# Recurrent blocks of a hybrid decoder layer: gates, recurrence and block end issued inside the next block's u projection, with the block's gate projection kept in another PSUM bank

## The chip, the cores and the metric

The kernel runs on one core of a Trainium2 chip. The metric is the device time of one execution in microseconds (us). The core has five engines with queues of their own: TensorE (PE in the profile, its weight loads PEld), VectorE (DVE), ScalarE (ACT), GpSimd (POOL) and SyncE (SP). Each works through its own instructions in order; semaphores hold an instruction back until what it reads is there, or until the place it writes is free. In this kernel SP's queue carries the loads of weights, POOL's the small transfers between stages.

## The reference

One layer over 16 meta positions and 1024 tokens, width 2048, all in float32. The input is normalized and multiplied by one wide matrix, the parts of which feed an attention branch and a recurrent branch; both are gated, joined, projected out, added to the input and normalized.

```python
h = rmsnorm(x, norm_g[l], NORM_EPS)
proj = jnp.einsum('btd,de->bte', h, w_in[l])
q, k, v, g_att, u, g_lru = jnp.split(proj, splits, axis=-1)
...
att = diff_attention(q, k, v, dist_bias, lam)           # softmax1 @ v - lam * softmax2 @ v, causal, 8 heads
att = (rmsnorm(att, subln_g[l], SUBLN_EPS) * (1.0 - lam_init)).reshape(B, T, D_ATTN)
att = att * jax.nn.silu(g_att)
rec = rg_lru_branch(u, ...)
rec = rec * jax.nn.silu(g_lru)
x = x + jnp.einsum('bte,ed->btd', jnp.concatenate([att, rec], axis=-1), w_out[l])
```

The recurrent branch works on 8 blocks of 128 channels:

```python
u = causal_depthwise_conv4(u, conv_w) + conv_b
r = jax.nn.sigmoid(u_block @ w_a + b_a)                 # gate r
i = jax.nn.sigmoid(u_block @ w_x + b_x)                 # gate i
a = jnp.exp(-LRU_C * r * jax.nn.softplus(-lru_lambda))
b = jnp.sqrt(-jnp.expm1(2.0 * log_a)) * i * u           # 1 in place of the root at t = 0
h[t] = a[t] * h[t - 1] + b[t]
```

## The kernel before

**Precision.** A float32 product is made of three fast matmuls. Each operand is split into a rounded high part and the rest (`split`, L77 to L80: the high part by ACT, the rest by DVE), and high x high, high x low and low x high are added up in PSUM. So each step over 128 rows of the contraction is a group of three matmuls (L158 to L160), and weights arrive as a load by SP (`wraw`, 2 buffers), a copy by ACT (`whi`, 3 buffers) and a subtraction by DVE (`wlo`, 3 buffers), each of half a column block (128 x 1024).

**Stages.** The sequence is worked in two halves: half A (meta positions and the first 512 tokens, 528 columns) and half B (512 columns). The stages follow each other on PE: attention of half A (8 heads, to about 450 us of the span), the 8 recurrent blocks of half A (to about 642 us, while POOL, ACT and DVE prepare the input of half B), attention of half B (to about 1141 us), the 8 recurrent blocks of half B (to about 1308 us), and the output projection.

**One head.** `head` (L225) projects q and k, makes scores (tag S, L339 and L341), takes the two softmaxes and their difference (L346 to L365, ending in DVE's L364), projects v and the gate, and then transposes the probabilities (L396, tag T), splits them (L400, L404) and multiplies by v into one bank, `pv` (L401 to L407). The bank is copied out (`att`, L413), its squares are summed by two matmuls into the same bank again (`ms`, L418 and L419), and the head ends in a store by POOL.

**One recurrent block.** `lru` (L523) gives two projections, u and gr, each 48 matmuls per column chunk (half A has two chunks for u, 272 and 256 columns). As soon as u is there, the sink `u_sink` (L450) calls `finish` (L464): four convolution steps on DVE (`uc`), the split into `uh` (ACT) and `ul` (DVE), the gate products (L485 to L487: 12 matmuls in half A, 6 in half B, into tags S and T), two sigmoids, a chain of ACT and DVE work, and the scan. After gr's 48 matmuls, `g_sink` (L509) scales it, takes its sigmoid, multiplies with the scan's result and stores by POOL.

**Order.** The Python code issues the blocks one after the other; a list scheduler with a model of the engines then sets the order on every engine from the dependences, and gives tiles their places when it issues them. `issue_after` holds what is issued within it behind an instruction on the same engine. `proj` (L135) has an argument `midway`: a function that is called before the ninth of the 16 groups of a chunk, with the rest of the chunk held behind the instruction that it returns. Before the change only the first head used it.

**PSUM.** Eight banks: tag S has 3, T has 2, proj has 2, and pv has 1. Before, u and gr of a recurrent block take tag proj (T in block 1 of half B), and pv lies idle while the recurrent blocks run.

## Time and profile before

| | |
|---|---|
| time, median of 3 runs | 1640.6 us (1637.65 to 1643.15) |
| profiled execution | 1637.0 us, of which the span is 1635.2 |
| TensorE busy | 1596.9 us, 98 % of the span, 8466 matmuls |
| DVE, ACT, POOL busy | 1117.6, 874.1, 205.2 us |
| mean granted TensorE clock | 0.995 |

The span runs from the first instruction to the last; the rest of the execution lies around it. Busy shares of PE count overlapping matmuls once. Since PE is busy nearly throughout, a stretch is read by its PE idle time: what PE waited for, where, and what the other engines did just before.

### The profile page before, as it was taken

What the parts mean: (1) busy time and instruction counts of PE and PEld (TensorE: products, weight loads), DVE (VectorE), ACT (ScalarE), POOL (GpSimd) and SP (SyncE); (2) the same over time, 40 slices, a digit from 0 to 9 for tenths busy, and PEclk for the clock granted to TensorE, in tenths of its full rate; (3) what the DMA queues carried; (4) which work ended last, traced back from release to release, by engine and by line L of the source; (5) the groups of instructions that cost most, each with busy time, mean ns of one, the idle gap of its engine ahead of it and who ended that gap; (6) DMA issues with size and microseconds to landing.
All of it is one profiled execution on the core that took longest, in us unless ns stands there. A gap on an engine that the chain in (4) does not pass through costs nothing.

```text
span 1635.2 us, 22985 instructions
## 1 busy us (share of the span) xinstructions
PE 1596.9 (98%) x8466; PEld 1370.8 (84%) x8466; DVE 1117.6 (68%) x2218; ACT 874.1 (53%) x1392; POOL 205.2 (13%) x308
## 2 busy tenths in 40 slices
PE   7999999999999999999999999999999999899996
PEld 6889889998989888888888888887887887788885
DVE  6766556665676667667668667757877656867996
ACT  5655555545566657456556556545776543332533
POOL 1211111110011010201011001000000002200262
PEclk9999999999999999999999999999999999999999
DMA  9633344333344443533234234233443388969874
GB/s 310 206 121 109 116 137 132 122 124 108 122 146 145 145 142 123 183 114 116 84 120 134 78 120 123 78 97 100 138 138 114 120 309 290 326 234 330 307 283 154
DMA packets 85196, 261.61 MB, mean 160 GB/s; under 512 B 11659, under 2 KB 13748, under 8 KB 84956
## 3 DMA queue, kind: packets, MB, share of 16 engines
q1 hardware_dynamic: 60544, 192.18, 35.2%
q0 software_dynamic: 24304, 67.90, 12.6%
q8 instruction: 67, 1.10, 0.3%
q14 instruction: 45, 0.37, 0.1%
q10 hardware_dynamic: 236, 0.06, 0.0%
HBM read 213.35 MB, written 39.86 MB: 155 GB/s over the span
## 4 chain that ended last, share of the span: by engine, by line
PE 75%; DVE 8%; issue 7%; DMA 7%; ACT 3%; POOL 1%; SPq 0%; ACTq 0%; DVEq 0%; POOLq 0%
PE proj L158 20%; PE proj L159 19%; PE proj L160 19%; PE T L396 2%; PE o L685 2%; PE o L686 2%; PE o L684 2%; DVE wlo L80 2%; PE S L341 2%; PE S L339 2%; DMA wb<-w_out 1%; DVE y L700 1%; DVE wb L658 1%; DMA xb<-mix_d 1%; DMA xt<-x 1%
## 5 line engine op out<-in xcount | busy, mean ns | idle before, releaser
L158 PE MATMUL proj<-hTA,whi 128*128 128x256 f32 (+2 forms) x1152 | 373.5, 325 | 1.9 <-ACT whi L79 1.9
L159 PE MATMUL proj<-hTA,whi 128*128 128x256 f32 (+2 forms) x1152 | 370.4, 322 | 0.0
L160 PE MATMUL proj<-hTA,wlo 128*128 128x256 f32 (+2 forms) x1152 | 369.5, 322 | 0.5 <-DVE wlo L80 0.5
L79 ACT ACTIVATE whi<-wraw 128x1024 fp32r<-128x1024 f32 (+1 forms) x218 | 228.2, 1047 | 244.8 <-PE proj L159 186.6
L80 DVE TENSOR_TENSOR wlo<-wraw,whi 128x1024 fp32r<-128x1024 f32 (+1 forms) x218 | 264.0, 1212 | 116.5 <-ACT whi L79 116.3
L158 PE MATMUL proj<-hTB,whi 128*128 128x512 f32 x768 | 302.1, 393 | 1.2 <-DVE gr L291 0.6
L160 PE MATMUL proj<-hTB,wlo 128*128 128x512 f32 x768 | 300.9, 392 | 0.0
L159 PE MATMUL proj<-hTB,whi 128*128 128x512 f32 x768 | 299.8, 390 | 0.0
L158 PEld LDWEIGHTS proj<-hTA,whi 128*128 128x128 f32 x1152 | 218.8, 190 | 18.7 <-ACT whi L79 2.6
L160 PEld LDWEIGHTS proj<-hTA,wlo 128*128 128x128 f32 x1152 | 218.7, 190 | 16.3 <-DVE wlo L80 0.7
L159 PEld LDWEIGHTS proj<-hTA,whi 128*128 128x128 f32 x1152 | 219.0, 190 | 14.4
L685 PE MATMUL o<-wlo,mix 128*128 128x512 f32 x416 | 163.2, 392 | 7.9 <-DVE wlo L80 7.9
L158 PEld LDWEIGHTS proj<-hTB,whi 128*128 128x128 f32 x768 | 144.3, 188 | 30.4 <-DVE gr L291 2.6
L160 PEld LDWEIGHTS proj<-hTB,wlo 128*128 128x128 f32 x768 | 144.2, 188 | 30.1
L159 PEld LDWEIGHTS proj<-hTB,whi 128*128 128x128 f32 x768 | 144.3, 188 | 28.6
L686 PE MATMUL o<-whi,mix 128*128 128x512 f32 x416 | 162.6, 391 | 0.0
L684 PE MATMUL o<-whi,mix 128*128 128x512 f32 x416 | 162.5, 391 | 0.0
L358 ACT ACTIVATE s<-s,st 128x144 f32<-128x144 f32 (+7 forms) x128 | 100.0, 782 | 50.9 <-DVE st L356 50.1
L685 PEld LDWEIGHTS o<-wlo,mix 128*128 128x128 f32 x416 | 78.4, 189 | 26.4 <-DVE wlo L80 10.0
L351 DVE TENSOR_SCALAR_CACHE_REDUCE s<-S,b 128x256 f32<-128x256 f32 (+5 forms) x176 | 82.6, 477 | 19.4 <-PE S L341 16.2
L684 PEld LDWEIGHTS o<-whi,mix 128*128 128x128 f32 x416 | 78.5, 189 | 16.6 <-ACT gate L488 0.3
L686 PEld LDWEIGHTS o<-whi,mix 128*128 128x128 f32 x416 | 78.5, 189 | 16.2
(240 smaller groups left out, 2357.6 us busy)
## 6 DMA issues: line engine op xcount, KB each, us to landing
wraw<-w_in SPq DMA_DIRECT2D x190, 512.0 KB, 4.0
wraw<-w_out SPq DMA_DIRECT2D x48, 512.0 KB, 4.3
mix<-mix_d SPq DMA_DIRECT2D x48, 256.0 KB, 5.1
wb<-w_out SPq DMA_DIRECT2D x24, 512.0 KB, 5.1
t_d<-wb POOLq DMA_DIRECT2D x16, 512.0 KB, 6.8
xb<-mix_d SPq DMA_DIRECT2D x24, 256.0 KB, 6.4
kk_d<-kk POOLq DMA_DIRECT2D x8, 528.0 KB, 3.0
kk<-kk_d POOLq DMA_DIRECT2D x8, 528.0 KB, 4.1
```

Of the source, the lines that this page charges most:

```text
L79: nc.scalar.activation(hi, src, AF.Copy)
L80: nc.vector.tensor_tensor(out=lo, in0=src, in1=hi.bitcast(F32), op=ALU.subtract)
L158: nc.tensor.matmul(ps[:, :n], lhsT=hi[:, c], rhs=xh, start=(kt == 0), stop=False)
L159: nc.tensor.matmul(ps[:, :n], lhsT=hi[:, c], rhs=xl, start=False, stop=False)
L160: nc.tensor.matmul(ps[:, :n], lhsT=lo[:, c], rhs=xh, start=False, stop=(kt == KT - 1))
L339: nc.tensor.matmul(ps[:, :w], lhsT=qq[:, j, qc], rhs=kk[:, j, c0:c0 + w], start=True, stop=False)
L341: nc.tensor.matmul(ps[:, :w], lhsT=self.qz[:, j, qc], rhs=kl[:, c0:c0 + w], start=False, stop=True)
L351: nc.vector.tensor_scalar(out=s[j][:, a:a + n], in0=ps[:, a - c0:a - c0 + n], scalar1=self.b31[:, h:h + 1], scalar2=-3.0e38, op0=ALU.add, ...
L358: nc.scalar.activation(s[j][:, :s_len], s[j][:, :s_len], AF.Exp, bias=nm[:, j:j + 1], accum_out=l[:, j:j + 1])
L684: nc.tensor.matmul(acc, lhsT=x[:, 0, tk], rhs=w[0], start=start, stop=False)
L685: nc.tensor.matmul(acc, lhsT=x[:, 0, tk], rhs=w[1], start=False, stop=False)
L686: nc.tensor.matmul(acc, lhsT=x[:, 1, tk], rhs=w[0], start=False, stop=stop)
```

## The change

`proj` now calls its `midway` function in the first of its chunks only. In `lru_part` the old `finish` is cut in two: `convolve` (convolution and split, still called as soon as u is there) and `recur` (gates, recurrence). `g_sink` now only keeps gr's bank, and a new `finish` runs `recur` and then what `g_sink` did; it returns the last gate matmul. The loops over blocks hand this `finish` as `midway` to the next block's u projection, so that a block's gates, recurrence and end are issued before the ninth group of the next u, and the rest of that u is held behind the last gate matmul. The last block's `finish` follows by itself. gr has to wait in PSUM for that long, and takes tag pv, which has one bank.

```diff
@@ -148,2 +148,3 @@
         for unit in work:
+            hook, midway = midway, None
             acc = [self.ps.tile([P, 512], F32, tag=j[3], name="proj", bufs={"S": 3, "pv": 1}.get(j[3], 2)) for _, j in unit]
@@ -151,4 +152,4 @@
                 for kt in range(KT):
-                    if kt == 8 and midway:
-                        order.enter_context(self.tc.issue_after(midway().ins))
+                    if kt == 8 and hook:
+                        order.enter_context(self.tc.issue_after(hook().ins))
                     c = slice((kt % 8) * P, (kt % 8) * P + P)
@@ -460,6 +461,6 @@
                 if c0 + w == n:
-                    state["h"] = finish()
+                    convolve()
             return f
-        def finish():
+        def convolve():
             ue = state["ue"]
@@ -476,2 +477,6 @@
                 nc.vector.tensor_copy(out=carry[:, 0:3], in_=ue[:, n:n + 3])
+            state["u"] = uc, uh, ul
+
+        def recur():
+            uc, uh, ul = state["u"]
             gates = []
@@ -486,3 +491,3 @@
                     nc.tensor.matmul(ps[:, :w], lhsT=wh, rhs=ul[:, c], start=False, stop=False)
-                    nc.tensor.matmul(ps[:, :w], lhsT=wl, rhs=uh[:, c], start=False, stop=True)
+                    last = nc.tensor.matmul(ps[:, :w], lhsT=wl, rhs=uh[:, c], start=False, stop=True)
                     nc.scalar.activation(o[:, c], ps[:, :w], AF.Sigmoid, bias=par[:, 5 + g:6 + g])
@@ -506,5 +511,11 @@
                 nc.vector.tensor_copy(out=carry[:, 3:4], in_=d[:, n - 1:n])
-            return d
+            state["h"] = d
+            return last
         def g_sink(ps):
+            state["g"] = ps
+
+        def finish():
+            last = recur()
+            ps = state["g"]
             sg = pool.tile([P, HALF], F32, tag="sg", name="sg", bufs=1)
@@ -519,6 +530,8 @@
             self.emit_mix(half, H + b, sg)
+            return last
+
+        return u_sink, g_sink, finish
-        return u_sink, g_sink
+    def lru(self, b, half, pool, tl, hT, tag="proj"):
-    def lru(self, b, half, pool, tl, hT, tag="proj", g_tag="proj"):
         gw = self.lru_weights(b, pool)
@@ -528,6 +541,6 @@
             self.carry[b] = self.carry_all[:, 4 * b:4 * b + 4]
-        us, gs = self.lru_part(b, half, pool, tl, gw, self.carry[b])
+        us, gs, finish = self.lru_part(b, half, pool, tl, gw, self.carry[b])
         chunks = [(0, HALF)] if half else [(0, 272), (272, 256)]
         return ((M_U + b, [(hT, c0, w, tag, us(c0, w)) for c0, w in chunks]),
-                (M_GR + b, [(hT, 0 if half else META, HALF, g_tag, gs)]))
+                (M_GR + b, [(hT, 0 if half else META, HALF, "pv", gs)]), finish)
@@ -853,5 +866,7 @@
             step, squares, fin_b = self.prep(pb, nc.gpsimd, self.xb, HALF, 1, hTB, LA, 2)
+            finish = None
             for b in range(8):
-                for m, jobs in self.lru(b, 0, pool, pool, hTA):
-                    self.proj((m, jobs))
+                u, g, then = self.lru(b, 0, pool, pool, hTA)
+                for m, jobs in (u, g):
+                    self.proj((m, jobs), midway=finish if m < M_GR else None)
                     if m < M_GR:
@@ -861,2 +876,4 @@
                             squares(b)
+                finish = then
+            finish()
             fin_b()
@@ -876,5 +893,7 @@
         with tc.tile_pool(name="lruB", bufs=1, side="left", reuse_waits="tile") as pool:
+            finish = None
             for b in range(8):
-                for m, jobs in self.lru(b, 1, pool, tl, hTB, *("T" if b == 1 else "proj",) * 2):
-                    self.proj((m, jobs))
+                u, g, then = self.lru(b, 1, pool, tl, hTB, "T" if b == 1 else "proj")
+                for m, jobs in (u, g):
+                    self.proj((m, jobs), midway=finish if m < M_GR else None)
                     if 1 <= b < 5:
@@ -883,2 +902,4 @@
                                 mixA.append(self.load_mix(m1, 0, len(mixA)))
+                finish = then
+            finish()
         tail.close()
```

The lines of the changed kernel are some lines further down (the projection's three matmuls are L159 to L161, the gates L490 to L492, the transposes L397, ms L419 and L420). Three places show what the scheduler makes of it.

First, PE at the gates of a block in the middle of half A (block 4 of 8, counted from 0). Before, the gates stand behind six matmuls of what follows (`proj<-hTA_1...` is group 1 of 16), first the four with `uh`, then those with `ul`:

```order
L159 MATMUL proj<-hTA_1_177,whi 128x272
L160 MATMUL proj<-hTA_1_161,wlo 128x272
L485 MATMUL S<-uh,lwh 128x272
L485 MATMUL S<-uh,lwh 128x256
L485 MATMUL T<-uh,lwh 128x272
L485 MATMUL T<-uh,lwh 128x256
L158 MATMUL proj<-hTA_2_162,whi 128x272
L159 MATMUL proj<-hTA_2_178,whi 128x272
L160 MATMUL proj<-hTA_2_162,wlo 128x272
L486 MATMUL S<-ul,lwh 128x272
```

In the changed kernel they stand behind 24 matmuls of the next block's u (`hTA_7` is group 7), twelve in a row:

```order
L159 MATMUL proj<-hTA_7_167,whi 128x272
L160 MATMUL proj<-hTA_7_183,whi 128x272
L161 MATMUL proj<-hTA_7_167,wlo 128x272
L490 MATMUL S<-uh,lwh 128x272
L491 MATMUL S<-ul,lwh 128x272
L492 MATMUL S<-uh,lwl 128x272
L490 MATMUL S<-uh,lwh 128x256
L491 MATMUL S<-ul,lwh 128x256
L492 MATMUL S<-uh,lwl 128x256
L490 MATMUL T<-uh,lwh 128x272
```

So the gates come 18 matmuls of 272 columns later after gr than before, and nothing else stands among them.

Second, PE at the end of the last attention head of half B. `s_10793` and `s_10821` are the probabilities of the last two of four row tiles, `proj<-hTB_15` is the end of block 0's u, and `hTB_0` to `hTB_2` in the piece of before are the start of its gr:

```order
L159 MATMUL proj<-hTB_15_4896,whi 128x512
L160 MATMUL proj<-hTB_15_4880,wlo 128x512
L158 MATMUL proj<-hTB_0_4865,whi 128x512
L159 MATMUL proj<-hTB_0_4881,whi 128x512
L160 MATMUL proj<-hTB_0_4865,wlo 128x512
L158 MATMUL proj<-hTB_1_4866,whi 128x512
L159 MATMUL proj<-hTB_1_4882,whi 128x512
L160 MATMUL proj<-hTB_1_4866,wlo 128x512
L158 MATMUL proj<-hTB_2_4867,whi 128x512
L159 MATMUL proj<-hTB_2_4883,whi 128x512
L396 MATMUL T<-ident,s_10793 16x128
L160 MATMUL proj<-hTB_2_4867,wlo 128x512
```

Now:

```order
L160 MATMUL proj<-hTB_15_4896,whi 128x512
L161 MATMUL proj<-hTB_15_4880,wlo 128x512
L397 MATMUL T<-ident,s_10793 16x128
L397 MATMUL T<-ident,s_10740 128x128
L397 MATMUL T<-ident,s_10765 128x128
L397 MATMUL T<-ident,s_10793 128x128
L397 MATMUL T<-ident,s_10821 16x128
L397 MATMUL T<-ident,s_10821 128x128
L402 MATMUL pv<-pm,vv 128x512
L406 MATMUL pv<-pth,vv 128x512
```

Before, the 48 matmuls of gr stand among the transposes of the last two row tiles; in the changed kernel gr uses the bank that pv and ms still hold, and stands only after the gates of block 0. Nothing but attention is left on PE from here to the last pv.

Third, ACT between the last pv and block 0's gates in half B. `pth_11091` is the split of the squares that ms reads, `sq_11090` a logarithm of ms, `uh_11191` what the gates read, `mix_...` a stored half-A result loaded back by SP and split. Before:

```order
L79 ACTIVATE mix_11386<-mix_11386 128x512
L79 ACTIVATE pth_11091<-sq_11090 128x512
L79 ACTIVATE mix_11390<-mix_11390 128x512
L79 ACTIVATE lwh_11118<-lw_11116 128x256
L79 ACTIVATE mix_11462<-mix_11462 128x512
L79 ACTIVATE mix_11466<-mix_11466 128x512
L79 ACTIVATE whi_11477<-wraw_11476 128x1024
L79 ACTIVATE mix_11571<-mix_11571 128x512
L79 ACTIVATE mix_11575<-mix_11575 128x512
L79 ACTIVATE lwh_11287<-lw_11285 128x256
L79 ACTIVATE whi_11483<-wraw_11482 128x1024
L79 ACTIVATE uh_11191<-uc_11186 128x512
```

Now:

```order
L79 ACTIVATE pth_11082<-T_11080 128x128
L414 ACTIVATE att_11089<-pv_10993 128x512
L79 ACTIVATE whi_11269<-wraw_11268 128x1024
L79 ACTIVATE pth_11091<-sq_11090 128x512
L79 ACTIVATE mix_11364<-mix_11364 128x512
L79 ACTIVATE mix_11368<-mix_11368 128x512
L79 ACTIVATE lwh_11118<-lw_11116 128x256
L79 ACTIVATE mix_11433<-mix_11433 128x512
L79 ACTIVATE mix_11437<-mix_11437 128x512
L422 ACTIVATE sq_11090<-eg_10583 128x512
L79 ACTIVATE uh_11191<-uc_11186 128x512
```

The splits of `mix` and of gate weights (`lwh`) stand ahead of `uh` in both; `whi_11269`, which takes the place of the first half of block 1's u weights, now stands ahead of `pth_11091`. The loads on SP that go with it (`wraw` are weights, `mix` the stored results), before:

```order
L118 DMA wraw_11394<-w_in 128x1024
L118 DMA wraw_11400<-w_in 128x1024
L118 DMA wraw_11476<-w_in 128x1024
L619 DMA mix_11386<-mix_d0_0_119 128x512
L619 DMA mix_11390<-mix_d0_1_120 128x512
L619 DMA mix_11462<-mix_d0_2_121 128x512
```

And SP in the changed kernel:

```order
L118 DMA wraw_11372<-w_in 128x1024
L632 DMA mix_11364<-mix_d0_0_119 128x512
L632 DMA mix_11368<-mix_d0_1_120 128x512
L118 DMA wraw_11378<-w_in 128x1024
L632 DMA mix_11433<-mix_d0_2_121 128x512
L632 DMA mix_11437<-mix_d0_3_122 128x512
```

So `mix_11433` is now loaded behind `wraw_11378`, which takes the buffer of `wraw_11268`, the source of `whi_11269` and of the `wlo` beside it. On PE the two `ms` matmuls and the gates now follow the 24th matmul of block 1's u, with nothing between them.

## Rows read from the trace of the kernel before

**Rows 1.** Page, busy time of each engine over the whole execution

```profile
PE 1596.9 (98%) x8466; PEld 1370.8 (84%) x8466; DVE 1117.6 (68%) x2218; ACT 874.1 (53%) x1392; POOL 205.2 (13%) x308
```

**Rows 2.** Busy time by stretch: width, PE, PEld, DVE, ACT, POOL, clock, DMA share, GB/s

```profile
1117.00:1160.00 43.00, 41.63 (x197) 33.30 (x196) 28.73 (x50) 24.39 (x38) 2.19 (x4) 1.00 0.37 121
```

**Rows 3.** Waits of PE over the whole span: total us, times, longest

```profile
PE S L485 <- ACT uh L79: 3.9, 4, 2.2
...
PE S L486 <- DVE ul L80: 0.7, 3, 0.2
```

**Rows 4.** Order of time on PE, gates of block 4, half A: start, duration, releaser

```profile
561.27 0.29 PE L159 MATMUL proj<-hTA,whi 128*128 128x272 f32 x1
561.39 0.28 PE L160 MATMUL proj<-hTA,wlo 128*128 128x272 f32 x1
563.84 0.51 PE L485 MATMUL S<-uh,lwh 128*128 128x272 f32 x2 [2.16 <-ACT uh L79]
```

**Rows 5.** Order of time on ACT, the same place

```profile
561.16 1.06 ACT L200 ACTIVATE xt<-xt 128x1024 f32<-128x1024 f32 x1 [1.53 <-DMA xt<-x]
...
562.21 1.04 ACT L79 ACTIVATE whi<-wraw 128x1024 fp32r<-128x1024 f32 x1
563.16 0.63 ACT L79 ACTIVATE uh<-uc 128x528 fp32r<-128x528 f32 x1
```

**Rows 6.** Busy time by stretch, around the gates of block 4

```profile
561.30:563.80 2.50, 0.38 (x4) 0.16 (x2) 2.05 (x5) 2.50 (x5) 0.00 (x0) 1.00 0.00 0
...
564.80:568.30 3.50, 3.28 (x16) 3.12 (x15) 2.83 (x5) 3.49 (x7) 0.00 (x0) 0.51 0.51 167
```

**Rows 7.** Order of time on PE, one gate wait of half B

```profile
1237.83 0.74 PE L485 MATMUL S<-uh,lwh 128*128 128x512 f32 x2 [1.05 <-ACT uh L79]
```

**Rows 8.** Order of time, all engines, start of the first recurrent block, half A

```profile
452.11 0.40 PE L158 MATMUL proj<-hTA,whi 128*128 128x512 f32 x1
...
452.19 1.06 ACT L79 ACTIVATE whi<-wraw 128x1024 fp32r<-128x1024 f32 x1 [1.12 <-PE proj L159]
...
453.49 1.22 DVE L80 TENSOR_TENSOR wlo<-wraw,whi 128x1024 fp32r<-128x1024 f32 x1
```

**Rows 9.** Order of time, all engines, last softmax of half B to its pv

```profile
1120.27 0.39 PE L158 MATMUL proj<-hTB,whi 128*128 128x512 f32 x1
...
1124.12 1.30 DVE L364 SCALAR_TENSOR_TENSOR s<-s,st,s 128x1040 f32<-128x1040 f32 x1
...
1130.75 0.38 PE L396 MATMUL T<-ident,s 128*16 128x128 f32 x2
...
1131.42 0.39 PE L159 MATMUL proj<-hTB,whi 128*128 128x512 f32 x1
...
1131.65 0.40 PE L160 MATMUL proj<-hTB,wlo 128*128 128x512 f32 x1
...
1133.01 0.50 PE L401 MATMUL pv<-pm,vv 80*128 80x512 f32 x1 [0.96 <-DVE pm L88]
```

**Rows 10.** Order of time, all engines, end of the last pv to ms

```profile
1146.16 0.28 PE L407 MATMUL pv<-pth,vv 128*128 128x128 f32 x1
...
1146.47 0.60 ACT L413 ACTIVATE att<-pv 128x512 f32<-128x512 f32 x1 [4.90 <-PE pv L407]
...
1147.11 0.69 DVE L414 TENSOR_TENSOR sq<-att 128x512 f32<-128x512 f32 x1 [3.94 <-ACT att L413]
...
1148.84 1.22 DVE L80 TENSOR_TENSOR wlo<-wraw,whi 128x1024 fp32r<-128x1024 f32 x1
...
1150.53 0.83 SPq L619 DMA_DIRECT2D mix<-mix_d  x2
...
1150.88 0.62 ACT L79 ACTIVATE pth<-sq 128x512 fp32r<-128x512 f32 x1
...
1151.70 0.74 DVE L470 SCALAR_TENSOR_TENSOR uc<-ue,lru_par_sb,uc 128x512 f32<-128x512 f32 x1
...
1154.81 1.23 ACT L79 ACTIVATE mix<-mix 128x512 fp32r<-128x512 f32 x2 [0.49 <-DMA mix<-mix_d]
```

## The prediction, made before the changed kernel was run

> **What bounds the kernel now.** I read the page first: TensorE is busy 98 % of the span and the other engines far less [rows 1], so a change in the order can only win or lose the time in which PE stands still. The windows by stage come next: from the last scores of half B to the first gates PE is busy 41.63 of 43.00 us, at a clock of 1.00 [rows 2]. Then the waits of PE: the gate matmuls wait 3.9 us for `uh` in four places (the longest 2.2) and 0.7 us for `ul` in three [rows 3]. The order of time shows how the longest arises. After the last u matmul at 561.39 nothing is issued until the first gate matmul at 563.84 [rows 4]. On ACT, which works in order, a square of `xt` and a weight copy `whi`, 1.06 and 1.04 us, stand ahead of `uh` [rows 5]. So the gates are ready to run about two microseconds too early in PE's order, six matmuls into the next u.
>
> **The gates in the steady blocks.** The change puts them behind 24 matmuls of the next u, 18 later than before. By rows 4 a wait of 2.45 us from issue to issue is the worst; 18 matmuls of 272 columns, at 0.12 us from issue to issue (561.27 to 561.39 [rows 4]), are 2.2 us. `uh` also stands ahead of the square on ACT then, and the waits for `ul`, 0.2 us at most, vanish with it. In half B the gates move behind 24 matmuls of 0.23 us (1131.42 to 1131.65 [rows 9]), 5.5 us, where the one wait in the rows was 1.05 [rows 7]. I take all 4.6 us of rows 3 as gone. Issue to issue a wait costs a little more than the view shows (2.45 less one matmul of 0.12 is 2.33, where it says 2.16), 0.16 over seven waits: 1.1 more.
>
> With the longest wait goes something else. In the 3.5 us from 564.80 the granted clock is 0.51, which is 1.2 GHz of the two levels, after 2.45 us with hardly a matmul at 1.00 [rows 6]; half of the work is lost there, 3.5 x (1 - 0.51) = 1.7 us. The sum of the gain: 4.6 + 1.1 + 1.7 = **7.4 us**; should `uh` still be late in half A's worst block, as rows 4 leave 0.1 us open, it is less by the price of that. The steady blocks pay nothing for the bank: gr's result is read by the first DVE instruction behind gr (the multiplication that gives `gx`, no longer behind the scan's chain in the order), and the next gr comes a whole u later.
>
> **The start of the recurrent blocks, half A.** Block 0's gr can't follow its u any more, since pv and ms of the last head hold the bank. PE goes on with block 1's u instead, whose first weights take the buffer of the half that PE has just finished. In the row of before that same copy starts at 452.19 and takes 1.06, the subtraction beside it ends at 453.49 + 1.22 = 454.71, and PE would have been through at 452.11 [rows 8]. In that time PE can run four u matmuls of 0.12 and one ms matmul of 0.23, 0.7 us in all. Of the 2.6 us to 454.71 it loses **1.9**. Before, gr's weights lay ready. At the other ends (the last block of half A, and of half B before the output projection) the gates follow the 48 matmuls of gr at once, 11 us after u, and `uh` has long been made: 0. POOL's store of a block's result moves half a u later, and the loads queued behind it on POOL feed work that PE needs only in the next stage: 0.
>
> **The end of attention, half B.** This is the dear part. Before, the last head's softmax, its transposes and its pv products had 48 matmuls of gr among them; now these are blocked by the bank, and of block 1's u only the first 24 may run before block 0's gates.
> - PE has finished block 0's u and can go to the transposes at 1120.27; the four that it can do take under half a microsecond, to about 1120.7. The last difference of softmaxes ends at 1124.12 + 1.30 = 1125.42 [rows 9]. Wait: 4.7.
> - From the last small transposes to the first pv product pass 1133.01 - 1130.75 = 2.26 us, in which ACT and DVE copy and split. Before, three gr matmuls filled a part, so PE lost 1133.01 - 1131.65 less one matmul of 0.23, that is 1.13 [rows 9]. Now one transpose is left to fill it: 2.0, so +0.9. The rest of the pv chain waits as before.
> - After the last pv product follow six u matmuls, 1.4 us. For ms come, by the rows of before: a gap of 0.31 to `att`, 0.60, `sq` 0.69 with its gap of 0.04, which is 1.6; then the weight copy `whi` that now stands ahead, 1.06, which starts only when the six u matmuls are through (1.8), ends at 2.9; then `pth`, 0.62 [rows 10]: 3.5 after the last pv, so PE waits 2.1. The second ms matmul needs `ptl`, behind `wlo` (1.22), a convolution step (0.74) and itself as long as `sq` (0.69) [rows 10]: at 2.9 + 2.65 = 5.5; with ms's first matmul done at 3.7 PE waits another 1.8.
> - The gates need `uh`. Ahead of it on ACT stand splits of stored half-A results. The load of the third stands on SP behind a weight load that needs the buffer free, so after `wlo` at 4.1; before, such a pair was issued at 1150.53 and used at 1154.81, 4.28 us later [rows 10]. That gives 4.1 + 0.4 + 4.3 = 8.8; two splits take 1.23, a logarithm and `uh` 0.6 each: 11.2. PE is through with ms at 5.7 and waits 5.5, and 0.2 for `ul`, as the waits of before had at most [rows 3].
>
> The sum is 4.7 + 0.9 + 2.1 + 1.8 + 5.5 + 0.2 = **15.2 us**. Of these I can bound the last: if the load were there at once, ACT and DVE alone (four splits of 0.6, `lwh` 0.4, the chain of ms behind `ptl`) bring `uh` at about 9.4, and PE waits 3.7. Upward nothing in the rows bounds the load; I allow 1 us. So 13.4 to 16.2.
>
> **The clock after such waits.** No row shows a wait of 4.7 or 5.5 us in the middle of PE's work. After 2.45 us with little work the level fell to 1.2 GHz for 3.5 us and cost 1.7 [rows 6]; after the gap of 1.36 us at 1131.65 [rows 9] the window shows no fall [rows 2]. By these I take one full price for the gates' wait, 1.7, and 0.7 for the softmax's wait, since the pv chain behind it stands partly on ACT and DVE anyway: **2.4**, with 0 and 5.1 (three times 1.7) as ends.
>
> The Trainium skill, "TensorE: Matmul & The Clock Gate", section "HAM oscillation — how this bites in real kernels", says that matmuls behind an idle gap start cold, and that the loss is half of the throttled time. The trace agrees: 0.51 for 3.5 us behind the gap. By that rule alone each of the two long waits costs the full 1.7, and the sum would be 1.0 higher.
>
> **Sum.** -7.4 + 1.9 + 15.2 + 2.4 = **+12.1 us** on the profiled execution's 1637.0, so 1649.1. The median of the three runs stands 3.6 above that execution; the prediction goes against the median: 1640.6 + 12.1 = **1652.7**.
>
> **Rivals.**
> 1. *The end of attention costs little, only the gate waits go.* If the softmax came earlier on DVE than in the row (its queue now holds nothing of gr's), or if PE found other work, only the gain and the 1.9 would be left: 1640.6 - 7.4 + 1.9 = 1635.1. For it: the gain's rows are measured, the loss is worked out. Against it: the softmax's end is set by ACT and DVE alone (DVE at 1124.12 has one weight split ahead of it), and the order on PE has nothing else to issue. It ends on the faster side if the sum of the waits there stays under 5.5 - 4.9 = 0.6 us. **0.07.**
> 2. *Gain and loss balance.* The waits at the end of attention sum to 5 to 10 us where I have 15.2, and the clock doesn't fall: -7.4 + 1.9 + 5 to 10 is -0.5 to 4.5, so 1640 to 1645. For it: each wait of that stretch is as long as a chain on ACT, DVE and SP that I put together from single rows, and what waits for one thing shortens the wait for the next. Against it: even with the load there at once it is 13.4. **0.15.**
> 3. *Cold clock throughout.* If the level falls behind each of the three groups of waits and the matmuls at 1.2 GHz push the pv chain onto PE: +5.1 instead of 2.4, and up to 2 more in the first blocks whose splits run late: 1656 to 1658. **0.18.**
> 4. *The single bank stalls each block*, if `gx` were late behind other work on DVE. 14 blocks of 0.5 us would give +7 more, 1660. The order speaks against it: `gx` stands right behind gr. **0.03.**
>
> The forecast itself, 1648 to 1656, has **0.57**.
>
> **Range and chances.** The bounds of the parts give 1640.6 + (-7.4 + 1.9 + 13.4 + 0) = 1648.5 to, with the gain less its clock (5.7), 1640.6 + (-5.7 + 1.9 + 16.2 + 5.1) = 1658 for the likeliest; to leave out no more than 2 in 10, and with part of the balance, the range is 1641 to 1660. A measurement tells 0.3 %, 4.9 us, from no change. Rival 1 is faster or just on the line: faster 0.06. Rival 2 is for most of its part within: same 0.14, with a little of rival 1. The rest is slower: 0.80.
>
> **What would show it.** In the changed kernel's profile the waits of PE for `uh` in the blocks of half A are gone, and no half clock stands near 565. At the start of half A's blocks a wait for `whi` and one for `wlo`, about 1 us each. Around 1120 a wait of the transposes for DVE's softmax difference of 4 to 5 us; before ms one for `pth` of about 2 and one for `ptl`; before block 0's gates in half B a wait for `uh` of 4 to 6 us, with ACT's split of `mix` released by a DMA; a clock near 0.5 behind. It is wrong if PE's waits from the last scores of half B to block 0's gates sum to less than 8 us, or if new waits show in the steady blocks.

## The result, and the profile after

The changed kernel takes 1653.9 us (median of 5 runs, 1649.9 to 1659.1) where the kernel before takes 1640.6 (5 runs, 1634.3 to 1643.2). The ratio is 1.0093, 95 % interval 1.0072 to 1.0115: slower, by 13.3 us at the medians and 15.3 by the ratio; 12.1 were forecast. The profiled execution took 1656.4 us, where 1649.1 was forecast.

The page's line of busy times and its line of the granted clock in 40 slices; TensorE does the same 8466 matmuls as in [rows 1] in a longer span, and one slice, from 1117 to 1158 us, shows a clock of 0.7:

```profile
PE 1603.8 (97%) x8466; PEld 1376.3 (83%) x8466; DVE 1119.3 (68%) x2218; ACT 871.3 (53%) x1389; POOL 204.6 (12%) x308
...
PEclk9999999999999999999999999997999999999999
```

The waits of PE over the whole span (us in total, times, longest), which answer to [rows 3]:

```profile
...
PE S L490 <- ACT uh L79: 5.3, 1, 5.3
PE T L397 <- DVE s L365: 4.6, 1, 4.6
PE ms L419 <- ACT pth L79: 4.4, 2, 3.0
PE proj L159 <- ACT whi L79: 2.5, 3, 1.0
PE pv L402 <- DVE pm L88: 1.8, 1, 1.8
PE ms L420 <- DVE ptl L80: 1.6, 1, 1.6
...
PE S L491 <- DVE ul L80: 0.7, 1, 0.7
```

Of the seven gate waits of before, one for `uh` of 5.3 us and one for `ul` of 0.7 are left; neither stands where one stood before. New are the transposes' wait for the last difference of softmaxes, and two waits of ms, 1.4 us for `pth` and 1.6 for `ptl`; the other 3.0 of the row of `pth` lie near 107 us, where the kernel before waits as long. All the long new ones lie in one stretch, from the last scores of half B to block 0's gates. PE there, in order of time (start, duration), first behind block 0's u, then behind the 24th matmul of block 1's u; these answer to [rows 9, 10]:

```profile
1119.57 0.60 PE L397 MATMUL T<-ident,s 128*16 128x128 f32 x4
1124.79 0.59 PE L397 MATMUL T<-ident,s 128*16 128x128 f32 x2 [4.63 <-DVE s L365]
1127.16 0.80 PE L402 MATMUL pv<-pm,vv 80*128 80x512 f32 x1 [1.77 <-DVE pm L88]
```

```profile
1142.79 0.39 PE L161 MATMUL proj<-hTB,wlo 128*128 128x512 f32 x1
1144.62 0.50 PE L419 MATMUL ms<-pth,ones 128*128 128x512 f32 x1 [1.44 <-ACT pth L79]
1146.69 0.50 PE L420 MATMUL ms<-ptl,ones 128*128 128x512 f32 x1 [1.57 <-DVE ptl L80]
1152.46 1.22 PE L490 MATMUL S<-uh,lwh 128*128 128x512 f32 x2 [5.28 <-ACT uh L79]
```

What the gates wait for is seen on ACT. `uh` stands behind four splits of `mix`, and the second pair waits 4.22 us for its load:

```profile
1142.99 1.06 ACT L79 ACTIVATE whi<-wraw 128x1024 fp32r<-128x1024 f32 x1 [0.60 <-PE proj L160]
1143.95 0.61 ACT L79 ACTIVATE pth<-sq 128x512 fp32r<-128x512 f32 x1
1144.47 1.13 ACT L79 ACTIVATE mix<-mix 128x512 fp32r<-128x512 f32 x2
1145.51 0.40 ACT L79 ACTIVATE lwh<-lw 128x256 fp32r<-128x256 f32 x1
1150.13 1.24 ACT L79 ACTIVATE mix<-mix 128x512 fp32r<-128x512 f32 x2 [4.22 <-DMA mix<-mix_d]
1151.28 0.61 ACT L422 ACTIVATE sq<-eg 128x512 f32<-128x512 f32 x1
1151.80 0.61 ACT L79 ACTIVATE uh<-uc 128x512 fp32r<-128x512 f32 x1
```

On SP that load was issued at 1145.89, right behind the weight load that had waited for its buffer until `wlo` was made (it ended at 1144.15 + 1.22, the first row here, of DVE):

```profile
1144.15 1.22 DVE L80 TENSOR_TENSOR wlo<-wraw,whi 128x1024 fp32r<-128x1024 f32 x1
1145.39 0.33 SPq L118 DMA_DIRECT2D wraw<-w_in  x1
1145.89 0.79 SPq L632 DMA_DIRECT2D mix<-mix_d  x2
```

Behind the waits the clock is down. Windows of the same core (width, then busy us of PE, PEld, DVE, ACT, POOL, then the clock): from 1117 to 1143, with the softmax's wait in it, it is 0.87 in the mean, which is as much as 6.8 us at half; from 1148 to 1158.5 it is 0.51, and the gates and the first u matmuls, which start at 1152.46, run at 1.2 GHz for 6 us:

```profile
1117.00:1143.00 26.00, 19.52 (x89) 14.85 (x87) 13.20 (x26) 12.12 (x21) 1.13 (x2) 0.87 0.21 68
...
1148.00:1158.50 10.50, 6.04 (x14) 4.75 (x15) 7.60 (x14) 8.25 (x13) 1.63 (x3) 0.51 0.33 116
1158.50:1165.00 6.50, 6.50 (x30) 5.33 (x30) 2.67 (x3) 3.58 (x5) 0.54 (x1) 1.00 0.08 23
```

To compare the kernels below by stretch I sum, over a stretch's matmuls, the time to the next one's start less what the shape takes at full speed in these traces (0.227 us at 512 columns, 0.124 at 272, 0.120 at 256, 0.108 for a transpose). This "loss" holds waits and clock together; it comes from one profile of each kernel, and where nothing is lost rounding can leave it a little under zero. The middle stretch ends 12 us behind the first gate matmul; e5's 21 extra matmuls count there as work. The second profile of the kernel before shows by how much the loss of one kernel can differ. The experiments ran beside the kernel before on chips of their own, so two of them are compared by their ratios to it.

| kernel | median us | ratio to before (95 %) | half A's blocks | end of attention B to gates | half B's blocks |
|---|---|---|---|---|---|
| before | 1640.6 | | 6.6 | 3.0 | 2.4 |
| before, second profile | 1637.7, one run | | 5.9 | 3.0 | 2.9 |
| changed | 1653.9 | 1.0093 (1.0072 to 1.0115) | 4.7 | 22.1 | -0.2 |
| e1, gr 0 of B free | 1649.9 | 1.0059 (1.0041 to 1.0077) | 1.9 | 19.9 | 0.4 |
| e2, gr 0 of A and B free | 1649.4 | 1.0050 (1.0033 to 1.0068) | 0.0 | 19.7 | 0.4 |
| e3, mix loads later | 1653.1 | 1.0078 (1.0056 to 1.0100) | 1.9 | 19.1 | 2.3 |
| e4, no hold | 1654.4 | 1.0085 (1.0060 to 1.0111) | 2.0 | 20.7 | -0.2 |
| e5, fill | 1651.2 | 1.0061 (1.0040 to 1.0083) | 1.9 | 16.4 | 2.6 |
| e6, both | 1640.8 | 0.9999 (0.9986 to 1.0011) | 1.9 | 7.9 | 1.2 |
| e7, blocks 0 and 1 as before | 1641.7 | 1.0000 (0.9987 to 1.0013) | 0.0 | 3.0 | 10.1 |
| e8, half A alone | 1635.9 | 0.9969 (0.9956 to 0.9982) | 3.5 | 3.0 | 2.5 |
| e9, half A alone, gr 0 free | 1633.0 | 0.9965 (0.9952 to 0.9978) | 0.0 | 3.0 | 2.1 |
| e10, half B alone | 1656.4 | 1.0116 (1.0097 to 1.0135) | 7.2 | 21.6 | 2.0 |

### The profile page after: what moved, and what is told of

Same layout as the page of the kernel before. It is cut to its first block, busy times and chain, and to the rows that moved or that the text cites. A ratio compares the mean times of both kernels' runs of the same rounds, so it can differ in the third digit from the quotient of the medians.

```text
span 1654.5 us, 22969 instructions
## 1 busy us (share of the span) xinstructions
PE 1603.8 (97%) x8466; PEld 1376.3 (83%) x8466; DVE 1119.3 (68%) x2218; ACT 871.3 (53%) x1389; POOL 204.6 (12%) x308
## 4 chain that ended last, share of the span: by engine, by line
PE 81%; DMA 6%; DVE 5%; issue 5%; ACT 2%; POOL 1%; SPq 0%; ACTq 0%; DVEq 0%; POOLq 0%
PE proj L159 18%; PE proj L161 18%; PE proj L160 18%; PE o L698 5%; PE o L699 5%; PE o L697 5%; PE T L397 2%; PE S L342 2%; PE S L340 2%; DMA wraw<-w_in 1%; PE pv L406 1%; PE pv L407 1%; PE pv L408 1%; DVE wlo L80 1%; DVE wb L671 1%
## 5 line engine op out<-in xcount | busy, mean ns | idle before, releaser
L159 PE MATMUL proj<-hTA,whi 128*128 128x256 f32 (+2 forms) x1152 | 373.8, 325 | 2.5 <-ACT whi L79 2.5
L161 PE MATMUL proj<-hTA,wlo 128*128 128x256 f32 (+2 forms) x1152 | 369.9, 322 | 1.0 <-DVE wlo L80 1.0
L159 PE MATMUL proj<-hTB,whi 128*128 128x512 f32 x768 | 302.5, 394 | 0.7 <-DVE gr L292 0.2
L161 PE MATMUL proj<-hTB,wlo 128*128 128x512 f32 x768 | 301.1, 392 | 0.0
L159 PEld LDWEIGHTS proj<-hTA,whi 128*128 128x128 f32 x1152 | 219.1, 190 | 19.4 <-ACT whi L79 3.5
L161 PEld LDWEIGHTS proj<-hTA,wlo 128*128 128x128 f32 x1152 | 218.8, 190 | 17.0 <-DVE wlo L80 1.5
L160 PEld LDWEIGHTS proj<-hTA,whi 128*128 128x128 f32 x1152 | 219.3, 190 | 15.4 <-DVE hTA L191 0.9
L161 PEld LDWEIGHTS proj<-hTB,wlo 128*128 128x128 f32 x768 | 144.7, 188 | 30.3
L159 PEld LDWEIGHTS proj<-hTB,whi 128*128 128x128 f32 x768 | 144.7, 188 | 30.2 <-DVE gr L292 2.1
L352 DVE TENSOR_SCALAR_CACHE_REDUCE s<-S,b 128x256 f32<-128x256 f32 (+5 forms) x176 | 82.8, 477 | 14.9 <-PE S L342 12.8
```

The costliest lines, as they stand in the source:

```text
L159: nc.tensor.matmul(ps[:, :n], lhsT=hi[:, c], rhs=xh, start=(kt == 0), stop=False)
L160: nc.tensor.matmul(ps[:, :n], lhsT=hi[:, c], rhs=xl, start=False, stop=False)
L161: nc.tensor.matmul(ps[:, :n], lhsT=lo[:, c], rhs=xh, start=False, stop=(kt == KT - 1))
L352: nc.vector.tensor_scalar(out=s[j][:, a:a + n], in0=ps[:, a - c0:a - c0 + n], scalar1=self.b31[:, h:h + 1], scalar2=-3.0e38, op0=ALU.add, ...
```

## The experiments

**e1: block 0's gr of half B away from the pv bank.**

```diff
-                u, g, then = self.lru(b, 1, pool, tl, hTB, "T" if b == 1 else "proj")
+                u, g, then = self.lru(b, 1, pool, tl, hTB, "T" if b == 1 else "proj", "pv" if b else "proj")
```

(`lru` gets back its argument `g_tag`, here with `pv` as default.)

> The changed kernel, but block 0's gr in half B goes to the tag proj again (one of its two banks) instead of the single pv bank; nothing else is edited. Theory (the loss is gr's 48 matmuls missing as work between the last head's softmax and ms): the waits of PE for the softmax difference (4.6 us), for pm (1.8) and most of the clock loss behind them go; the waits between the last pv and the gates shrink less, since the order still puts ms and the gates directly behind 24 matmuls of block 1's u. The stretch from the last scores to block 1's gr loses 6 to 10 us instead of 22; time about 1640 to 1646. Rival (the loss is the hold of block 1's u behind block 0's gates, wherever gr lies): the waits at ms and uh keep their 9 us and the time stays within 6 us of the changed kernel's 1653.9. Second rival (the loss lies in the output projection, where the profile of the changed kernel lost 3.6 us more): no change of more than 3 us.

Measured: 1649.9, by the ratio 5.6 us less than the changed kernel (0.0034 of 1640.6), where 8 to 14 were expected. The waits of PE in the stretch:

```profile
PE S L490 <- ACT uh L79: 8.3, 1, 8.3
PE ms L419 <- ACT pth L79: 3.9, 1, 3.9
PE pv L402 <- DVE pm L88: 1.0, 1, 1.0
```

The wait for the softmax difference is gone, as expected; but ms and the gates now wait 3.9 and 8.3 us, more than in the changed kernel. ACT shows why:

```profile
1143.83 1.28 ACT L525 ACT_TABLE_LOAD   x1
1145.12 0.63 ACT L525 ACTIVATE sg<-gx 128x512 f32<-128x512 f32 x1
...
1152.38 1.28 ACT L422 ACT_TABLE_LOAD   x1
1153.68 0.63 ACT L422 ACTIVATE sq<-eg 128x512 f32<-128x512 f32 x1
1154.33 1.28 ACT L423 ACT_TABLE_LOAD   x1
1155.62 0.63 ACT L423 ACTIVATE sq<-sq 128x512 f32<-128x512 f32 x1
...
1156.82 0.61 ACT L79 ACTIVATE uh<-uc 128x512 fp32r<-128x512 f32 x1
```

gr is there early, so its sigmoid `sg` (L525) comes into ACT's order ahead of `pth` and of the logarithm, with a load of its function table; the logarithm and the exponential of the old head then each need a table load again, 1.28 us apiece, and `uh` stands behind all three. The kernel before has the same three loads (at 1148.53, 1160.42 and 1162.37), but there `uh` starts at 1159.79, ahead of the last two, and PE has gr and block 1's u to work on. My expectation had counted the filler and not what gr's end puts on ACT ahead of `uh`. The clock stays at half for 17 us of such waits, and 19.9 us are lost there, where 6 to 10 were expected. So the bank alone isn't the cause; the rival, that the hold costs as much wherever gr lies, is nearer to what was measured.

**e2: the same in both halves.**

```diff
-                u, g, then = self.lru(b, 0, pool, pool, hTA)
+                u, g, then = self.lru(b, 0, pool, pool, hTA, g_tag="pv" if b else "proj")
```

> As the run before, and block 0's gr of half A in the tag proj again too. Theory: at the start of half A's blocks the wait for whi (1.2 us), for wlo (0.65) and the half clock behind them (1.5) go as well, so 3 us less than the run with half B alone: about 1637 to 1643. Rival (the loads of weights at that place are late in any order): within 1 us of the run with half B alone.

Measured: 1649.4; 1637 to 1643 were expected, a figure that stood on e1's and missed with it. The loss of half A's blocks is 0.0. The profile shows the 2 us gone; between medians half a microsecond is within the noise, so the times don't settle it. e9 repeats this edit in another company.

**e3: stored half-A results loaded two blocks later.**

```diff
-                    if 1 <= b < 5:
+                    if 3 <= b < 7:
```

> The changed kernel, but the stored half-A results are loaded and split in blocks 3 to 6 of half B instead of 1 to 4; the order on PE is the same. Theory (uh waits behind splits of mix on ACT, whose load stands on SP behind a weight load): the wait of the gates for uh falls from 5.3 us to 1 to 3, and with it part of the half clock behind; 3 to 6 us less, about 1648 to 1651. Rival (uh waits for the chain through ms on ACT and DVE, not for the load): the wait stays above 4 us and the time within 1.5.

The first wait for `uh` falls from 5.3 to 2.4, as the theory said:

```profile
PE S L490 <- ACT uh L79: 3.0, 2, 2.4
```

By the ratio the time is 2.5 less, but the intervals overlap, so it doesn't tell the theory's 3 to 6 from the rival's 1.5. The loss in the stretch falls by 3.0; half B's later blocks lose 2.5 more, among it a second wait for `uh`, 0.6 us, at the last block. So some 3 us of the first wait hung on the load. What is left of it hangs on the chain through ms, which the rival named: ACT stands idle for 3.45 us until DVE has read ms for the logarithm ahead of `uh`. Most of what was won in the stretch was lost again later.

**e4: block 1's u not held.**

```diff
-                    self.proj((m, jobs), midway=finish if m < M_GR else None)
+                    self.proj((m, jobs), midway=finish if m < M_GR and b != 1 else None)
+                    if b == 1 and m < M_GR:
+                        finish()
```

(in half B's loop.)

> The changed kernel, but in half B block 0's gates and end are issued after the whole u of block 1 instead of in its middle, so that its 48 matmuls aren't held; gr of block 0 still waits for the pv bank. Theory (bank and hold each cost their part): the second half of block 1's u, 24 matmuls of 0.23 us or 5.5 us, fills the waits at ms and a part of that at uh; the waits for the softmax difference (4.6) and pm (1.8) stay. 5 to 7 us less than the changed kernel, about 1647 to 1649. Rival (all of it is the hold): down to 1638. Rival (all of it is the bank): no change of more than 2 us.

Measured: 1654.4, no change that can be told. The second half of u does fill the waits at ms and most of that at `uh`. Then PE meets the bank: block 0's gr waits for the old head's last reading of ms, 2.81 us, and runs at half clock:

```profile
1150.46 0.73 PE L490 MATMUL S<-uh,lwh 128*128 128x512 f32 x2 [0.97 <-ACT uh L79]
1152.54 0.50 PE L491 MATMUL S<-ul,lwh 128*128 128x512 f32 x1 [1.34 <-DVE ul L80]
...
1156.54 0.79 PE L159 MATMUL proj<-hTB,whi 128*128 128x512 f32 x1 [2.81 <-DVE eg L425]
```

5 to 7 us less were expected. The time reads like the rival "all of it is the bank", but e1, which frees the bank and wins only 5.6, rules that out.

**e6: both at once** (the edits of e1 and e4).

```diff
-                u, g, then = self.lru(b, 1, pool, tl, hTB, "T" if b == 1 else "proj")
+                u, g, then = self.lru(b, 1, pool, tl, hTB, "T" if b == 1 else "proj", "pv" if b else "proj")
...
+                    if b == 1 and m < M_GR:
+                        finish()
```

> Both at once: block 0's gr in half B in tag proj, and block 1's u not held (block 0's gates and end issued after it); either alone left 20 us of loss in the stretch from the last scores on. Theory (PE is without work there for two reasons in a row, first gr's bank, then the hold, and the chain over ACT that makes uh is longer when gr's sigmoid and the table loads it brings stand in it): with both gone 96 matmuls fill the stretch; what stays is a wait for uh and for the bank of block 1's gr of 3 to 4 us and a part of the clock loss. 6 to 10 us lost there in place of 22; time 1637 to 1643. Rival (the chain over SP and ACT that ends in uh sets the end whatever fills it): above 1648.

Measured: 1640.8, by the ratio 15.4 us less than the changed kernel, where e1 alone gave 5.6 and e4 nothing that can be told. The longest waits left in the stretch are for block 2's weights:

```profile
PE proj L161 <- DVE wlo L80: 1.9, 1, 1.9
PE pv L402 <- DVE pm L88: 1.0, 1, 1.0
PE proj L159 <- ACT whi L79: 0.8, 1, 0.8
```

So two things stand in a row: gr lacks its bank, and what could run in its place is held. Taking away one leads PE to the other. The three table loads of e1 stand ahead of `uh` here too (at 1146.22, 1155.36 and 1157.30), and no gate waits more than 0.5 us: the chain on ACT costs little where PE has other work. By the table the stretch still loses 4.9 more than in the kernel before, and the blocks of the two halves lose 5.9 less: the time is that of before because the two nearly balance.

**e5: filler ahead of block 0's gates.**

```diff
+            if half and b == 0:
+                junk = self.ps.tile([P, 512], F32, tag="S", name="S", bufs=3)
+                with self.tc.issue_after(self.last_ms.ins):
+                    for i in range(21):
+                        fill = nc.tensor.matmul(junk, lhsT=self.ones, rhs=fill_rhs[0], start=(i == 0), stop=(i == 20))
```

(`last_ms` is the second matmul of ms, `fill_rhs` 512 columns of the input; the lines that hand them over are left out.)

> The changed kernel with 21 extra matmuls of 512 columns between ms and block 0's gates in half B; their products go to a free bank and are read by nobody. They are 21 x 0.23 = 4.8 us of work in the wait of 5.5 us and move nothing else on PE. Theory (the level of 1.2 GHz behind that wait costs half of the 6 us of gates and u matmuls that run at it): the gates run at 2.4 GHz, the wait ends at the same time, and the stretch loses 3 us less; about 1651. Rival (what runs at the lower level waits for other engines anyway): the same time as the changed kernel within 1 us. If the fill delayed the gates, the time would rise by up to the 4.8 us.

Measured: 1651.2, the time that was expected, but not on the way that was expected. The fill itself began, at 1143.73, at the lower level, and the gates came 37.5 us behind the last scores in place of 35.4. They then ran in a window at full clock:

```profile
1141.80:1146.00 4.20, 2.87 (x7) 2.29 (x8) 4.20 (x9) 0.56 (x2) 0.54 (x1) 0.50 0.68 216
1146.00:1151.00 5.00, 5.00 (x18) 3.98 (x17) 3.62 (x7) 4.40 (x8) 0.54 (x1) 0.74 0.17 58
1151.00:1157.00 6.00, 6.00 (x29) 4.95 (x28) 2.51 (x5) 4.89 (x7) 1.08 (x2) 1.00 0.26 87
```

From the first gate matmul the next 20 take 4.5 us here and 7.5 in the changed kernel: the clock behind the wait costs 2.9 us, as the theory had it, but the fill ran over by 2.1, so 0.9 us was won in this stretch. (The 16.4 of the table is lower by the 4.8 us of the fill itself, which it counts as work.) The rest of the difference, 2.8 us between the medians and 5.2 by the ratios, whose intervals overlap, is not shown to be the fill's: at half A's start, for one, this profile has no half clock and the changed kernel's has. The 2.9 is about half of the 6 us that ran at 0.51. The Trainium skill, "TensorE: Matmul & The Clock Gate", section "HAM oscillation — how this bites in real kernels", counts half of the throttled time as lost. The 2.9 agrees with that.

**e7: blocks 0 and 1 of half B, and block 0 of half A, in the tags of before; the rest as changed.**

```diff
-                u, g, then = self.lru(b, 1, pool, tl, hTB, "T" if b == 1 else "proj", "pv" if b else "proj")
+                u, g, then = self.lru(b, 1, pool, tl, hTB, "T" if b == 1 else "proj", ("proj", "T")[b] if b < 2 else "pv")
```

(on top of e6, with e2's edit.)

> As the run with bank and hold, and also block 1's gr of half B in tag T as before the change, and block 0's gr of half A in tag proj: the steady blocks as in the changed kernel, both starts as before it. Theory: the stretch at the end of attention loses 3 to 4 us as before the change, half A's blocks lose 6 us less than before the change and half B's 2 less: 1631 to 1635, faster than the kernel before by 6 to 9. Rival (the gain in the steady blocks is taken back in the output projection, which lost 15 to 17 us in each profile with the change against 12.9 before): 1637 to 1641, no faster than before.

Measured: 1641.7, the rival's number, not by the rival's reason. The end of attention is as before, 3.0. But half B's blocks lose 10.1: at the start of block 3's gr PE waits 0.7 us for the multiplication `gx` that empties the pv bank of block 2's, then 2.2 for weights, whose split stands behind a scan on DVE; in a later block 2.9 for `uh`:

```profile
PE S L490 <- ACT uh L79: 2.9, 1, 2.9
PE proj L161 <- DVE wlo L80: 2.4, 2, 2.2
...
PE proj L159 <- DVE gx L523: 0.7, 1, 0.7
```

The edit touched blocks 0 and 1; the order that the scheduler made of the later blocks changed with them (gr of block 3 now starts behind 24 matmuls of its u, ahead of the gates).

**e8: the change in half A alone.** `lru_m` is the changed kernel's `lru`; half B keeps the old one.

```diff
-                for m, jobs in self.lru(b, 0, pool, pool, hTA):
-                    self.proj((m, jobs))
+                u, g, then = self.lru_m(b, 0, pool, pool, hTA)
+                for m, jobs in (u, g):
+                    self.proj((m, jobs), midway=finish if m < M_GR else None)
```

> The change in half A alone; half B's blocks are issued as in the kernel before. Theory: the gate waits of half A go (6 us less), the start of half A's blocks loses 2 to 3.5 (weights' split, and the half clock behind it in one of the profiles): 2 to 5 us less than before, 1636 to 1639. Rival (half A's gain is no gain): within 1 us of 1640.8. Rival (half A costs as much as it gives and more): above 1642.

Measured: 1635.9, 0.31 % faster than before (0.18 to 0.44), as the theory said. What is left is the start: waits for `whi` and `wlo`, and a half clock behind them.

```profile
PE proj L159 <- ACT whi L79: 1.0, 1, 1.0
PE proj L161 <- DVE wlo L80: 0.4, 1, 0.4
```

**e9: e8 with block 0's gr in tag proj** (e2's edit).

```diff
-                u, g, then = self.lru_m(b, 0, pool, pool, hTA)
+                u, g, then = self.lru_m(b, 0, pool, pool, hTA, g_tag="pv" if b else "proj")
```

> As the run with the change in half A alone, and block 0's gr of half A in tag proj instead of the pv bank; half B as in the kernel before. Theory: the 2.1 us that the start of half A's blocks still lost go, 6.6 us less than before the change in all: 1633 to 1636, the fastest of all kernels here. Rival (the start's 2 us come back elsewhere, since each of the last variants lost in a place that the edit did not touch): 1636 to 1638, no faster than half A alone.

Measured: 1633.0, 0.35 % faster than before (0.22 to 0.48) and the fastest of all kernels here. No wait is left in half A's blocks:

```profile
PE S L340 <- DMA qq<-qf: 1.9, 1, 1.9
```

The one row is the first scores of half B, which wait 1.9 us for a transfer of `qq`, so part of the gain is lost again there. The intervals of e8 and e9 overlap: the edge over e8 isn't settled.

**e10: the change in half B alone.** e8's edit in the other loop, half A as before.

```diff
-                for m, jobs in self.lru(b, 1, pool, tl, hTB, *("T" if b == 1 else "proj",) * 2):
-                    self.proj((m, jobs))
+                u, g, then = self.lru_m(b, 1, pool, tl, hTB, "T" if b == 1 else "proj")
+                for m, jobs in (u, g):
+                    self.proj((m, jobs), midway=finish if m < M_GR else None)
```

> The change in half B alone; half A's blocks are issued as in the kernel before. Theory (the halves add up): the changed kernel is 13.3 over the kernel before, half A alone 4.5 under it, so half B alone costs 16 to 19: 1656 to 1659. Rival (the halves share something, such as the placing of weights in buffers): under 1654.

Measured: 1656.4, 17.1 over before. With e8's 4.3 under, the halves add up to 12.8; the changed kernel is 13.3 over. By the ratios it is 13.9 and 15.3. The halves add up within the noise, as the theory said.

**The kernel before once more**, without an edit.

> The kernel before once more, for a second profile. In eight profiles with some form of the change the output projection lost 14 to 17 us, in the one of before 12.9. Theory (the stage varies from execution to execution, and that one was a quick one): this profile loses 14 us or more there, with a time of 1639 to 1644. Rival (the change costs 2 to 4 us in the output projection): 13 us or less again.

Measured: 1637.7, with a loss of 13.4 in the output projection: between the two theories. The profiles of all kernels lie from 11.6 to 17.2 there, and 11.6 is e10's, which has all of half B's cost. The loss in that stage doesn't follow the edits; that some of the changed kernel's 16.5 is due to it can't be ruled out by one profile of each.

## Why the prediction was right, point by point

- **Steady gates.** Forecast -7.4 for both halves. By the loss, half A's steady blocks went from 6.5 to 1.0 and half B's from 2.4 to -0.2: -8.1. Right in kind, 0.7 more in size. I had set the half clock at block 4 among it, and it is gone. But the second profile of the kernel before has a wait of 1.7 us at the same gates, where the first has 2.2, and no half clock behind it, so the price of the clock there is not lost in every execution.
- **Start of half A.** Forecast 1.9. PE waited for `whi` and `wlo` as described, at the very instants of [rows 8]:

```profile
453.26 0.40 PE L159 MATMUL proj<-hTA,whi 128*128 128x272 f32 x1 [1.03 <-ACT whi L79]
...
454.72 0.39 PE L161 MATMUL proj<-hTA,wlo 128*128 128x272 f32 x1 [0.44 <-DVE wlo L80]
```

1.03 and 0.44 by the rows; from issue to issue, less one matmul each, it is 1.8. What I left out is the clock behind it: 0.50 for the 3.4 us from 455.30, 1.7 us more. e8's profile shows it too; those of e1, e3, e4, e5 and e6, with the same waits, don't.

```profile
455.30:458.70 3.40, 3.40 (x17) 3.40 (x16) 2.25 (x4) 0.64 (x1) 0.00 (x0) 0.50 0.50 159
```

- **Last block of half A.** Forecast 0; in half A the gates waited 0.7 us for `ul`. e8 has no such wait at the same place. POOL's later stores were forecast at 0 too; the first scores of half B waited 1.2 us for `qq`, which POOL loads, where the two profiles of before show no such wait. That the stores are its cause is not shown.
- **End of attention, half B.** Forecast 4.7, 0.9, 2.1, 1.8, 5.5 and 0.2. From the rows after, issue to issue less the matmul's own time: 4.8, 2.1 less the 1.1 of before, 1.6, 1.8, 5.5, and 0.2 for `ul`, which can't be told from the half clock. Each wait stands behind the instruction that the prediction named, the DMA on SP too (e3). One reading was off without harm: [rows 2] end at 1160, and the first gates of before stand at 1164.7, with no wait of PE between.
- **The clock.** Forecast 2.4: the mis-sized term. The gates' part was set at 1.7, from the one pattern at hand; it is 2.9 by e5. The five waits above sum to 15.8 and the pv chain's own waits of before to 1.9; of the 22.1 that leaves 1.5 for the clock in the pv chain, where I had 0.7. So 4.4 in the stretch, and the 1.7 at half A's start that wasn't foreseen.
- **Against it.** The steady blocks gained 0.7 more than forecast, which took back a part; the stretch at the end of attention lost 19.1 more than before where 15.2 + 2.4 were forecast.
- **The sum.** By the table the three stretches lose 14.6 more than before, not 12.1; the two profiled executions lie 19.4 apart, of which 3.6 are in the output projection (16.5 against 12.9) and 1.1 in half B's attention. The causes and most of the sizes were right. That 12.1 comes within 1.2 of the medians' 13.3 is in part luck: errors of both signs, and a spread between executions as large as they are.
- **Rivals.** That the wait at the end costs little fell by the rows, and with it the balance at 5 to 10 us: the waits there sum to 15.8, or 14.7 more than before. Of the cold clock throughout, the price of 5.1 is nearer to the 4.4 found than my 2.4; its 2 us more in the first blocks of half B didn't come. The single bank stalling each block shows nowhere in the changed kernel; once, with 0.7 us, in e7.

What the prediction didn't say is that bank and hold must both go. It named both, but priced the waits with gr simply missing; e1 and e4 show that taking away one brings a part or nothing.

## What to carry to other kernels

When the end of a block is put into the middle of the next, price the first block by itself: its work was the filler of the stage before, and an idle buffer may be in that stage's hands. Where two things keep the filler away, taking away one only leads to the other, so read what PE meets next before you count a gain. A change that helps one loop and hurts another of the same shape can be kept for the first alone.

## What the runs showed of the hardware that was not expected

The granted clock stayed at half in one piece across waits that came one after the other: [rows 6] show 3.5 us behind a single gap, the changed kernel 10.2 us from 1148.2, e1 17.1 us from 1145.7. So several waits close together cost more than the pattern behind one of them had shown, and the fill of e5, though it keeps PE busy, ran at the lower level itself for a part of its length. The same waits don't always bring the fall: behind 1.03 and 0.44 us at half A's start the level fell in the changed kernel and in e8, and in five other profiles it did not.
